# Rotary queries with channels on the partitions, their halves stacked by DMA

## The chip, the cores and the metric

The kernel runs on one core of a Trainium2 chip, in one launch. Its time is device microseconds; of several runs the median counts. Engines: PE (TensorE, matmuls and transposes), DVE (VectorE), ACT (ScalarE), POOL (GpSimd, here above all a queue of DMAs) and SP (SyncE, the other queue of DMAs). Each takes its instructions in the order in which they are written for it; they wait for one another by semaphores.

## The reference

Two layers of an encoder for 512 tokens of 2048 channels. Each layer normalises its input, projects it, and runs three kinds of head beside each other: latent attention (8 heads, 512 keys), a short gated convolution, and attention into 256 memory tokens (4 heads). What matters here is the rotary part of the latent queries, 64 channels of each head:

```python
def apply_rope(x, cos, sin):
    half = x.shape[-1] // 2
    x1, x2 = x32[..., :half], x32[..., half:]
    return jnp.concatenate([x1 * cos - x2 * sin, x2 * cos + x1 * sin], axis=-1)
...
q = (rmsnorm(q_lat, q_norm_g[l]) @ w_uq[l]).reshape(b, s, MLA_HEADS, QK_HEAD_DIM)
q = jnp.concatenate([q[..., :QK_NOPE_DIM],
                     apply_rope(q[..., QK_NOPE_DIM:], cos[:, :, None, :], sin[:, :, None, :])], axis=-1)
...
sc = jnp.einsum('bqhd,bkhd->bhqk', qi, k) * scale
m_out = memory_attention(q_mem, mem_n, w_mk[l], w_mv[l])
```

## The kernel before

All products are made in float32r; an operand that needs more bits is split in a high and a low part (`split_to`, L301: ACT casts the high part, the DVE subtracts it for the low part), and `mm3s` (L294) multiplies high by high, high by low and low by high: 12 matmuls for four blocks of channels and one PSUM bank.

The program is a list of Python steps (`add`, `put`) that are written one after the other. The order of PE, SP and POOL is that of the steps, by hand (L1488). The order of DVE and ACT is chosen by a scheduler when the program is built, except in the first steps and in the output projection. So a step that moves on PE moves what the scheduler makes of the other two.

`mixer` (L1124) writes, for each layer: the gates' transposes (tps, then y on ACT); in layer 0 beside them the keys and values of the memory (mk, mv, then Km, Vm); between these the rotary queries; then a pipeline (`pipeline`, L1104) of the four memory heads and the eight heads of latent attention. `head_iters` (L1029) gives each head four score tiles. A score tile goes: sc on PE, its negated maximum nm on the DVE (L1047), the exponential P on ACT (L1050), rec and the scaling of P, then three iterations later its transposes ptp on PE (L1067), the split into PT, and two iterations later the products o with the values (L298). Between the iterations stand the products of the next pair's queries (qps), keys (kps) and values (vps), with weights wh (ACT's cast, L212) and wl (DVE, L216).

The rotary queries (`q_rope_steps`, L918): for each of four token tiles t, `products(t)` makes a bank of 128 tokens x 512 (8 heads x 64 channels); `rot(t)` rotates it on the DVE (four rm of 128x256 with cos and sin, one sum, L946 to L950) and splits it into qs; `turn(t)` transposes qs on PE, eight 128x128 blocks (qrt, L971: a head's high part above its low part), and ACT copies them into the two tiles QR, four heads each (L973). `rot(2)` also has ACT compute an exponential of nothing (L960), so that the table of exponentials is loaded there (ACT_TABLE_LOAD) and not ahead of the first P. The rotary scores of latent attention read QR much later (L1043, L1044).

Buffers come in turn from pools: `raw` has 8 of 128x1024 f32 (4 KB a partition); the loaded weights (wr), rm and qs all take theirs from it. PSUM has 8 banks.

Of the kernel before, what the change touches and what calls it, by code (L numbers as in the profile page):

```python
# [5 lines left out]
F32 = mybir.dt.float32  # L6
# [3 lines left out]
ALU = mybir.AluOpType  # L10
# [241 lines left out]
def encoder(tc, x, mem, positions, pre_norm_g, w_in, q_norm_g, w_uq, kv_norm_g, w_ukv, conv_w,  # L252
# [665 lines left out]
    def q_rope_steps(l):  # L918
# [9 lines left out]
        units = [Unit(("qr", l, kp), [wl[:, 2 * kp + a, :, NOPE:] for a in range(2)], alloc=keep) for kp in range(2)]  # L928

        def products(t):  # L930
            def f(*ch):
                cH, cL = G["cq"]
                hi, lo = (a.rearrange("p (j c) -> p j c", j=4) for a in st["w"])
                ps = st["ps", t] = bank("qr")
                sl = slice(t * P, (t + 1) * P)
                mm3s([(ps, (cH[:, k, sl], cL[:, k, sl]), (hi[:, k, :], lo[:, k, :]), k == 0, k == 3, {})
                      for k in range(4)])
            return f

        def rotate(t, sc):  # L940
            q8 = st.pop(("ps", t)).rearrange("p (h s i) -> p h s i", h=HEADS, s=2)
            m1 = sc[:, :512].rearrange("p (h s i) -> p h s i", h=HEADS, s=2)
            m2 = sc[:, 512:].rearrange("p (h s i) -> p h s i", h=HEADS, s=2)
            cos, sin = G["cos2"][:, t], G["sin2"][:, t]
            for s in range(2):
                nc.vector.tensor_tensor(m1[:, :, s, :], q8[:, :, s, :],  # L946
                                        cos[:, s:s + 1, :].broadcast_to([P, HEADS, HALF]), op=ALU.mult)
                nc.vector.tensor_tensor(m2[:, :, s, :], q8[:, :, 1 - s, :],
                                        sin[:, s:s + 1, :].broadcast_to([P, HEADS, HALF]), op=ALU.mult)
            nc.vector.tensor_tensor(m1, m1, m2, op=ALU.add)  # L950
            return m1.rearrange("p h s i -> p h (s i)")

        def rot(t):
            def g():
                mr = rotate(t, raw_p.tile([P, 1024], F32, tag="raw", name=nm("rm")))
                qs = st["qs", t] = raw_p.tile([P, 1024], F32R, tag="raw", name=nm("qs")).rearrange(
                    "p (h s i) -> p h s i", h=HEADS, s=2)
                split_to(qs[:, :, 0, :], qs[:, :, 1, :], mr)
                if t == 2:
                    nc.scalar.activation(small(1, "nm"), mr[:, :1] if len(mr.shape) == 2 else mr[:, 0, :1], AF.Exp, scale=0.0)  # L960
            return g

        def turn(t):
            def g():
                if t == 0:
                    G["QR"] = [slab("QR", F32R).rearrange("p (h c) -> p h c", c=S) for _ in range(2)]
                qs = st.pop(("qs", t))
                for g4 in range(2):
                    pt = bank("qrt", F32R)
                    for h in range(4):  # L970
                        nc.tensor.transpose(pt[:, h * P:(h + 1) * P], qs[:, 4 * g4 + h].rearrange("p s i -> p (s i)"),  # L971
                                            G["identr"])
                    nc.scalar.copy(G["QR"][g4][:, :, t * P:(t + 1) * P],  # L973
                                   pt.bitcast(F32).rearrange("p (h c) -> p h c", h=4))
            return g
# [147 lines left out]

    def mixer(l, C, gates, pair2, tail):  # L1124

        rope, turns = q_rope_steps(l)
        if l == 0:
            ms = [(f, u, 1.0) for f, u, _ in mem_steps(l)]
            add(tables)
# [384 lines left out]
```

## Time and profile before

| | us |
|---|---|
| median of 3 runs | 1511.08 (1510.95 to 1511.76) |
| profiled execution | 1510.62 |
| its span, first to last instruction | 1508.8 |
| PE busy | 1485.1 (98%) |
| DVE busy | 1154.9 (77%) |
| ACT busy | 863.6 (57%) |
| POOL busy | 181.3 (12%) |

1.8 us of the profiled execution lie outside its span. The mean granted clock of PE over the span is 0.997 of full speed. The rotary queries of layer 0 are made from about 443 to 475 us, those of layer 1 from about 1192 to 1215 us. A row of a timeline gives the start of a run of like instructions and the time from its first start to its last end; matmuls overlap, so the time that a group holds PE is read from its start to the start of the next.

### The profile page before, as it was taken

The numbers are of one execution on the slowest core, as the hardware profiler recorded it, in microseconds if no ns is written. First come the engines' busy times: TensorE is split into PE (matmuls) and PEld (weight loads), VectorE is DVE, ScalarE is ACT, GpSimd is POOL, SyncE is SP. The second block draws the span as 40 slices with busy tenths as digits, with TensorE's granted clock in tenths as the row PEclk, the third lists the DMA queues.
The fourth block names the chain that finished last, engine by engine and source line by source line (L and its number), as shares of the span: only waits on it lengthen the run. The fifth ranks groups of instructions, "written<-read, shape, count | busy, mean of one in ns | idle before, by whom it ended". The sixth has DMA issues, their size and how long they took to land.

```text
span 1508.8 us, 20419 instructions
## 1 busy us (share of the span) xinstructions
PE 1485.1 (98%) x7613; PEld 1277.0 (85%) x7613; DVE 1154.9 (77%) x1516; ACT 863.6 (57%) x1327; POOL 181.3 (12%) x199
## 2 busy tenths in 40 slices
PE   8999999999999999999999999999999999999996
PEld 7878888997898888888888888888988888888875
DVE  5887877575887768888798877887686786698777
ACT  7743543454766768655498443534454686775534
POOL 0212020211000000021120112010221000002111
PEclk9999999999999999999999999999999999999998
DMA  8999695979565102399797899785978421127874
GB/s 308 226 219 220 188 193 165 193 198 239 164 212 166 43 29 68 94 214 283 220 343 230 225 231 225 199 179 156 207 198 202 158 76 37 43 89 147 283 177 128
DMA packets 144096, 270.64 MB, mean 179 GB/s; under 512 B 17160, under 2 KB 39788, under 8 KB 140780
## 3 DMA queue, kind: packets, MB, share of 16 engines
q1 hardware_dynamic: 108504, 190.10, 39.6%
q0 software_dynamic: 35360, 79.18, 27.0%
q8 instruction: 60, 0.98, 0.3%
q14 instruction: 40, 0.33, 0.1%
q10 hardware_dynamic: 132, 0.05, 0.0%
HBM read 254.61 MB, written 15.73 MB: 179 GB/s over the span
## 4 chain that ended last, share of the span: by engine, by line
PE 89%; DVE 3%; ACT 3%; DMA 2%; issue 2%; POOL 0%; DVEq 0%; POOLq 0%; ACTq 0%
PE P L298 62%; PE o L298 4%; PE mk L298 3%; PE mv L298 3%; PE qps L298 3%; PE ptp L1067 2%; PE tps L822 2%; PE vps L298 2%; PE qr L298 1%; PE kps L298 1%; PE sc L1039 1%; PE sc L1040 1%; PE sc L1045 1%; DMA wr<-in_w_in_dram 1%; PE sc L1044 1%
## 5 line engine op out<-in xcount | busy, mean ns | idle before, releaser
L212 ACT CAST wh<-wr 128x1024 fp32r<-128x1024 f32 (+1 forms) x404 | 413.5, 1031 | 449.3 <-PE P L298 258.9
L216 DVE TENSOR_TENSOR wl<-wr,wh 128x1024 fp32r<-128x1024 f32 (+1 forms) x404 | 479.1, 1194 | 223.2 <-ACT wh L212 219.2
L298 PE MATMUL P<-wh,S 128*128 128x512 f32 (+1 forms) x1792 | 444.9, 385 | 3.2 <-DVE S L435 1.5
L298 PEld LDWEIGHTS P<-wh,S 128*128 128x128 f32 x1792 | 334.3, 188 | 63.2 <-DVE S L435 1.9
L298 PE MATMUL P<-wh,A 128*128 128x512 f32 (+1 forms) x1312 | 325.8, 385 | 2.1 <-ACT wh L212 1.9
L298 PEld LDWEIGHTS P<-wh,A 128*128 128x128 f32 x1312 | 244.6, 188 | 47.5 <-ACT wh L212 3.2
L298 PE MATMUL P<-wl,S 128*128 128x512 f32 (+1 forms) x896 | 243.7, 384 | 0.0
L298 PEld LDWEIGHTS P<-wl,S 128*128 128x128 f32 x896 | 168.0, 188 | 30.5
L298 PE MATMUL P<-wl,A 128*128 128x512 f32 (+1 forms) x656 | 178.6, 384 | 0.1
L142 POOL DMA_DIRECT2D wr<-in_w_in_dram x84 | 101.7, 1212 | 550.2 <-DVE wl L216 458.8
L298 PEld LDWEIGHTS P<-wl,A 128*128 128x128 f32 x656 | 122.9, 188 | 22.6 <-DVE wl L216 0.5
L200 DVE TENSOR_TENSOR wr<-wr,wr 128x1024 f32<-128x1024 f32 (+1 forms) x100 | 118.9, 1191 | 10.1 <-DMA wr<-in_w_in_dram 7.9
L1050 ACT ACTIVATE P<-sc,nm 128x512 f32<-128x512 f32 (+1 forms) x96 | 59.8, 624 | 31.5 <-DVE nm L1047 30.8
L1047 DVE TENSOR_REDUCE nm<-sc 128x1 f32<-128x512 f32 (+1 forms) x96 | 57.0, 595 | 12.9 <-PE sc L1045 12.1
L303 DVE TENSOR_TENSOR PT<-ptp,PT 128x512 fp32r<-128x512 f32 (+1 forms) x96 | 56.6, 593 | 6.4 <-ACT PT L302 6.1
L142 POOL DMA_DIRECT2D wr<-in_w_o_dram x32 | 38.7, 1209 | 188.7 <-DVE wl L216 176.5
L1056 ACT ACTIVATE P<-P,rec 128x512 f32<-128x512 f32 (+1 forms) x80 | 53.9, 683 | 6.7 <-DVE rec L1052 6.7
L226 ACT ACTIVATE wh<-wr,cols 128x512 fp32r<-128x512 f32 x64 | 42.6, 715 | 21.5 <-PE mv L298 8.6
L302 ACT CAST PT<-ptp 128x512 fp32r<-128x512 f32 (+1 forms) x96 | 48.9, 521 | 9.3 <-PE ptp L1067 6.9
L298 PE MATMUL o<-PT,V 128*128 128x256 f32 x384 | 53.6, 289 | 0.0
L1067 PE MATMUL ptp<-identr,P 128*128 128x128 f32 x320 | 49.9, 272 | 0.8 <-ACT P L1056 0.7
L227 DVE SCALAR_TENSOR_TENSOR wl<-wr,cols,wh 128x512 fp32r<-128x512 f32 x64 | 45.2, 746 | 6.6 <-ACT wh L226 5.8
(256 smaller groups left out, 1758.2 us busy)
## 6 DMA issues: line engine op xcount, KB each, us to landing
wr<-in_w_in_dram SPq DMA_DIRECT2D x172, 512.0 KB, 4.5
wr<-in_w_o_dram SPq DMA_DIRECT2D x72, 512.0 KB, 4.1
wr<-in_w_in_dram POOLq DMA_DIRECT2D x68, 512.0 KB, 7.3
wr<-in_w_in_dram SPq DMA_DIRECT2D x40, 416.0 KB, 3.3
wr<-in_w_o_dram POOLq DMA_DIRECT2D x32, 512.0 KB, 7.7
wr<-in_w_mk_dram SPq DMA_DIRECT2D x16, 512.0 KB, 6.7
wr<-in_w_mv_dram SPq DMA_DIRECT2D x16, 512.0 KB, 5.8
wr<-in_w_in_dram POOLq DMA_DIRECT2D x16, 416.0 KB, 5.7
```

The lines of the kernel that those rows point to most:

```text
L142: engine.dma_start(dst, src, **kw)
L200: nc.vector.tensor_tensor(src, src, tiles[c], op=ALU.add)
L212: nc.scalar.copy(hi[:, :n], src)
L216: nc.vector.tensor_tensor(lo[:, :n], src, hi[:, :n].bitcast(F32), op=ALU.subtract)
L227: nc.vector.scalar_tensor_tensor(lo[:, h], src[:, h], g, hi[:, h].bitcast(F32), op0=ALU.mult, op1=ALU.subtract)
L298: nc.tensor.matmul(ps, a[turn[0]], b[turn[1]], start=first and turn == (0, 0), stop=last and turn == ((1, 0) if late == 0 else (0, 1)), **kw)
L302: nc.scalar.copy(hi, src)
L303: nc.vector.tensor_tensor(lo, src, hi.bitcast(F32), op=ALU.subtract)
L1047: nc.vector.tensor_reduce(nmax, ps, axis=AX.X, op=ALU.max, negate=True)
L1050: nc.scalar.activation(pt, ps, AF.Exp, bias=nmax, accum_out=tot)
L1056: nc.scalar.activation(pt, pt, AF.Copy, scale=rec)
L1067: nc.tensor.transpose(ps[:, k * P:(k + 1) * P], pt[:, k * P:(k + 1) * P], G["ident"])
```

## The change

A product bank now holds one half of the rotary channels (x = 0 the first 32 of a head's 64, x = 1 the last 32) of four heads (g = 0 or 1), 128 channels by 512 tokens: the weights are the stationary operand, the latent moves. There are again four banks of 12 matmuls a layer. `rot(g)` takes the two banks of a group of four heads and makes its two outputs, each with two products with a table, one sum or difference, and a split into qs, 128x512 throughout (L946 to L948, L303). The outputs lie with channels on the partitions already, so `turn` is gone; `stack(g)` brings high and low parts and the two halves into QR by DMA: for each x a copy of qs (512 KB) to DRAM (qsd, L963) and two reads of it into QR (256 KB each, L966), all on POOL's queue. The tables cos and sin are turned once in layer 0 (two copies on POOL, eight transposes on PE, two copies on ACT) and kept in DRAM (tabd) for layer 1, where SP loads them. The exponential of nothing moves to the end of `rot(1)` (L953). The rotary weights come in pieces of 32 channels, eight DMAs for four.

```diff
-        units = [Unit(("qr", l, kp), [wl[:, 2 * kp + a, :, NOPE:] for a in range(2)], alloc=keep) for kp in range(2)]
+        units = [Unit(("qr", l, kp), [wl[:, 2 * kp + a, :, NOPE + x * HALF:NOPE + (x + 1) * HALF] for a in range(2) for x in range(2)],
+                      alloc=keep) for kp in range(2)]
...
+        def products(g, x):
+            def f(*ch):
...
+                mm3s([(ps, (hi[:, k], lo[:, k]), (cH[:, k, :], cL[:, k, :]), k == 0, k == 3, {}) for k in range(4)], 0)
...
+        def rot(g):
+            def f():
+                one, two = st.pop(("ps", g, 0)), st.pop(("ps", g, 1))
+                cos, sin = st["tab"]
+                st["qs", g] = []
+                for a, b, op in ((one, two, ALU.subtract), (two, one, ALU.add)):
+                    m = raw_p.tile([P, 1024], F32, tag="raw", name=nm("rm"))
+                    nc.vector.tensor_tensor(m[:, :S], a, cos, op=ALU.mult)
+                    nc.vector.tensor_tensor(m[:, S:], b, sin, op=ALU.mult)
+                    nc.vector.tensor_tensor(m[:, :S], m[:, :S], m[:, S:], op=op)
+                    qs = raw_p.tile([P, 1024], F32R, tag="raw", name=nm("qs"))
+                    split_to(qs[:, :S], qs[:, S:], m[:, :S])
+                    st["qs", g].append(qs)
+                if g:
+                    nc.scalar.activation(small(1, "nm"), m[:, :1], AF.Exp, scale=0.0)
+            return f
+
+        def stack(g):
+            def f():
+                qr = slab("QR", F32R)
...
+                for x, qs in enumerate(st.pop(("qs", g))):
+                    d = dram.tile([P, 1024], F32, name=nm("qsd"))
+                    nc.gpsimd.dma_start(d, qs.bitcast(F32))
+                    for s in range(2):
+                        r = s * ROPE + x * HALF
+                        nc.gpsimd.dma_start(qr[r:r + HALF, :].rearrange("p (h c) -> p h c", c=S),
+                                            d[:, s * S:(s + 1) * S].rearrange("(h i) c -> i h c", i=HALF))
+            return f
...
-                    put(rope[q - 6], turns[q - 7:q - 6])
+                    put(rope[q - 6])
...
-            put(rope[2], turns[1:2], ms[14:15], rope[3], turns[2:3], ms[15:])
+            put(rope[2], stacks[:1], ms[14:15], rope[3], ms[15:], stacks[1:])
...
-                put([(g, []) for g in gates[2 * t:2 * t + 2]], rope[t])
-            put(turns[:1])
+                put([(g, []) for g in gates[2 * t:2 * t + 2]], rope[t], stacks[:1] if t == 2 else [])
+            put(stacks[1:])
...
-        for k, s in enumerate(turns[3:] if l == 0 else turns[1:]):
-            between[k] = between.get(k, []) + [s]
```

The rows that follow show the order of instructions on an engine; a name is a tile and its number, and the brackets name the semaphores waited for (DMASW: a DMA of POOL's queue has landed; DMAHW: one of SP's; else the engine).

The DVE in layer 1 before, around the first maximum of a memory score (nm_10647): rm_10584 and qs_10590 are token tile 2, rm_10620 is tile 3.

```order
L948 TENSOR_TENSOR rm_10584<-qr_10571,sin_3689 128x8x32
L950 TENSOR_TENSOR rm_10584<-rm_10584 128x512 [waits DVE_49]
L1047 TENSOR_REDUCE nm_10647<-sc_10643 128x1 [waits PE_49]
L303 TENSOR_TENSOR qs_10590<-rm_10584,qs_10590 128x8x64 [waits DVE_49,Activation_49]
L946 TENSOR_TENSOR rm_10620<-qr_10607,cos_3698 128x8x32 [waits DVE_49]
L948 TENSOR_TENSOR rm_10620<-qr_10607,sin_3689 128x8x32
```

The DVE in layer 1 after, at the same place (the first maximum is nm_10632): qs_10540 is output x = 1 of group 0, rm_10603 and qs_10607 are x = 0 of group 1, rm_10610 and qs_10614 its x = 1; wl_10751 are weights of the pair's keys and values.

```order
L303 TENSOR_TENSOR qs_10540<-rm_10536,qs_10540 128x512 [waits DMASW1_49,Activation_49]
L946 TENSOR_TENSOR rm_10603<-qr_10556,tab_10463 128x512 [waits DVE_49,PE_49]
L947 TENSOR_TENSOR rm_10603<-qr_10590,tab_10463 128x512 [waits PE_49]
L948 TENSOR_TENSOR rm_10603<-rm_10603 128x512 [waits DVE_49]
L216 TENSOR_TENSOR wl_10751<-wr_10355,wh_10750 128x1024 [waits DMAHW2_49,PE_49,Activation_49]
L303 TENSOR_TENSOR qs_10607<-rm_10603,qs_10607 128x512 [waits Activation_49]
L946 TENSOR_TENSOR rm_10610<-qr_10590,tab_10463 128x512 [waits DMASW4_49]
L947 TENSOR_TENSOR rm_10610<-qr_10556,tab_10463 128x512
L948 TENSOR_TENSOR rm_10610<-rm_10610 128x512 [waits DVE_49]
L1064 TENSOR_REDUCE nm_10632<-sc_10628 128x1
L303 TENSOR_TENSOR qs_10614<-rm_10610,qs_10614 128x512 [waits Activation_49]
```

The first maximum has moved behind the last rotation, and the second qs, the weights and the last rotation ahead of it wait for DMAs and for PE.

ACT in layer 1 before, from the table load to the first exponential of a score (P_10649).

```order
L960 ACT_TABLE_LOAD
L960 ACTIVATE nm_10593<-rm_10584 128x1 [waits DVE_49]
L973 CAST QR_10629<-qrt_10631 128x4x128 [waits PE_49]
L302 CAST qs_10590<-rm_10584 128x8x64 [waits PE_49]
L973 CAST QR_10630<-qrt_10637 128x4x128
L1050 ACTIVATE P_10649,tot_10650<-sc_10643,nm_10647 128x256 [waits DVE_49]
L302 CAST Q_10661<-qps_10662 128x512 [waits PE_49]
```

ACT in layer 1 after, up to the scaling of the first P (P_10634); L953 is the exponential of nothing.

```order
L302 CAST qs_10540<-rm_10536 128x512 [waits DMASW1_49,DVE_49,Activation_49]
L212 CAST wh_10750<-wr_10355 128x1024 [waits DMAHW2_49,PE_49]
L302 CAST qs_10607<-rm_10603 128x512 [waits DVE_49]
L302 CAST qs_10614<-rm_10610 128x512 [waits DVE_49,Activation_49]
L953 ACT_TABLE_LOAD
L953 ACTIVATE nm_10617<-rm_10610 128x1
L1067 ACTIVATE P_10634,tot_10635<-sc_10628,nm_10632 128x256 [waits DVE_49]
L1067 ACTIVATE P_10668,tot_10669<-sc_10662,nm_10666 128x256 [waits DVE_49]
L1073 ACTIVATE P_10634<-P_10634,rec_10637 128x256 [waits DVE_49]
```

The table load now stands behind the last qs cast, and the casts of Q, which stood between the first exponentials, come later.

POOL in layer 0 after, from the first copy of qs on: qs_3939 and qs_3946 are the two outputs of group 0, qs_4048 is the first of group 1.

```order
L963 DMA qsd_3983<-qs_3939 128x1024 [waits DMASW1_49,DVE_49]
L966 DMA QR_3982<-qsd_3983 32x4x512 [waits DMASW2_49,DMASW1_49,PE_49]
L966 DMA QR_3982<-qsd_3983 32x4x512 [waits DMASW3_49]
L963 DMA qsd_3987<-qs_3946 128x1024 [waits DMASW4_49,DVE_49]
L966 DMA QR_3982<-qsd_3987 32x4x512 [waits DMASW5_49,DMASW4_49]
L966 DMA QR_3982<-qsd_3987 32x4x512 [waits DMASW6_49]
L963 DMA qsd_4084<-qs_4048 128x1024 [waits DMASW7_49,DVE_49]
```

None of these DMAs was there before. The reads of a copy, which wait for its landing, stand ahead of the next copy in the same queue.

## Rows read from the trace of the kernel before

**Rows 1.** The page: busy time of each engine, and the chain that ended last.

```profile
PE 1485.1 (98%) x7613; PEld 1277.0 (85%) x7613; DVE 1154.9 (77%) x1516; ACT 863.6 (57%) x1327; POOL 181.3 (12%) x199
...
PE 89%; DVE 3%; ACT 3%; DMA 2%; issue 2%; POOL 0%; DVEq 0%; POOLq 0%; ACTq 0%
```

**Rows 2.** PE's waits, whole span (us in total, times, longest).

```profile
PE P L298 <- ACT wh L212: 2.8, 4, 0.9
...
PE ptp L1067 <- ACT P L1056: 0.7, 1, 0.7
```

**Rows 3.** Stretches: length, busy time (instructions) by engine, PE clock, DMA share, GB/s.

```profile
453.00:466.00 13.00, 13.00 (x81) 11.38 (x81) 8.25 (x15) 5.89 (x10) 0.41 (x5) 1.00 0.77 268
...
480.00:500.00 20.00, 19.30 (x140) 17.94 (x139) 18.81 (x55) 15.95 (x51) 0.00 (x0) 1.00 0.22 69
500.00:560.00 60.00, 60.00 (x361) 52.68 (x360) 39.16 (x74) 42.05 (x85) 0.00 (x0) 1.00 0.11 37
...
1219.00:1236.00 17.00, 16.92 (x124) 16.02 (x125) 15.99 (x48) 14.54 (x45) 0.00 (x0) 1.00 0.19 60
...
1485.00:1509.00 24.00, 11.27 (x50) 9.01 (x48) 16.37 (x24) 7.39 (x16) 4.44 (x6) 0.79 0.61 176
```

**Rows 4.** Timeline of PE, layer 1 (start, us, operation, repeats).

```profile
1198.70 1.03 PE L822 MATMUL tps<-identr,ga 128*128 128x128 f32 x8
...
1205.96 0.80 PE L971 MATMUL qrt<-identr,qs 128*128 128x128 f32 x8
1206.59 0.35 PE L1039 MATMUL sc<-Km,QmH 128*128 128x256 f32 x1
...
1219.24 0.95 PE L298 MATMUL o<-PT,Vm 128*128 128x256 f32 x6
```

**Rows 5.** Tiles rm, qs, QR: ns min/median/max, first to last start us.

```profile
L946 DVE TENSOR_TENSOR rm<-qr,cos x16: 410/416/426, 446.9 to 1209.0; 128x256 f32<-128x256 f32 x16
...
L303 DVE TENSOR_TENSOR qs<-rm,qs x8: 681/693/695, 450.4 to 1211.5; 128x512 fp32r<-128x512 f32 x8
...
L1043 PE MATMUL sc<-KAB,QR x64: 389/391/398, 497.3 to 1354.6; 128*128 128x512 f32 x64
```

**Rows 6.** Timelines of DVE and ACT, layer 1 ([idle before <- releaser]).

```profile
1201.78 0.69 DVE L303 TENSOR_TENSOR qs<-rm,qs 128x512 fp32r<-128x512 f32 x1 [0.74 <-ACT qs L302]
...
1207.21 0.42 DVE L1047 TENSOR_REDUCE nm<-sc 128x1 f32<-128x256 f32 x1 [2.49 <-PE sc L1045]
...
1215.31 1.23 DVE L216 TENSOR_TENSOR wl<-wr,wh 128x1024 fp32r<-128x1024 f32 x1 [0.77 <-ACT wh L212]
...
1204.06 1.28 ACT L960 ACT_TABLE_LOAD   x1
...
1207.93 0.49 ACT L1050 ACTIVATE P<-sc,nm 128x256 f32<-128x256 f32 x1
...
1214.19 1.09 ACT L212 CAST wh<-wr 128x1024 fp32r<-128x1024 f32 x1
...
1218.70 0.58 ACT L302 CAST K<-kps 128x512 fp32r<-128x512 f32 x1
1219.16 0.52 ACT L1056 ACTIVATE P<-P,rec 128x256 f32<-128x256 f32 x1
```

**Rows 7.** DMA issues (KB, median us to landing); landings of tiles xs and mTd.

```profile
xs<-xr POOLq DMA_DIRECT2D x8, 512.0 KB, 6.2
...
DMA to landing us min/median/max: 3.0/6.4/17.1
...
DMA to landing us min/median/max: 5.4/8.1/11.7
```

**Rows 8.** Timeline of PE, layer 0.

```profile
455.95 0.81 PE L971 MATMUL qrt<-identr,qs 128*128 128x128 f32 x8
...
479.53 0.38 PE L1067 MATMUL ptp<-identr,P 128*128 128x128 f32 x2
...
482.79 0.97 PE L298 MATMUL o<-PT,Vm 128*128 128x256 f32 x6
```

More of the change, by code (lines that the diff above doesn't have):

```diff
@@ L940, in rotate @@
[L940 to L975, printed above, removed]
@@ L976, in q_rope_steps @@
-        return [[(products(t), units if t == 0 else []), (rot(t), [])] for t in range(NT)], [(turn(t), []) for t in range(NT)]
+                hi, lo = (a.rearrange("p (k x g m) -> p k x g m", k=4, x=2, g=2)[:, :, x, g, :] for a in st["w"])
+                ps = st["ps", g, x] = bank("qr")
+                mm3s([(ps, (hi[:, k], lo[:, k]), (cH[:, k, :], cL[:, k, :]), k == 0, k == 3, {}) for k in range(4)], 0)
+            return f
+        def rot(g):
[14 more added lines that the diff above has]
+            return f
@@ new lines, in stack @@
+        def stack(g):
+            def f():
+                qr = slab("QR", F32R)
+                G["QR"] = G["QR"][:g] if g else []
+                G["QR"].append(qr.rearrange("p (h c) -> p h c", c=S))
+                for x, qs in enumerate(st.pop(("qs", g))):
[6 more added lines that the diff above has]
+            return f
@@ new lines, in tables_four @@
+        def tables_four():
+            if l:
+                tab = raw_p.tile([P, 1024], F32, tag="raw", name=nm("tab"))
+                nc.sync.dma_start(tab, G["tabd"])
+                st["tab"] = tab[:, :S], tab[:, S:]
+                return
+            st["four"] = [scrap(n) for n in ("cos4", "sin4")]
+            for v, src in zip(st["four"], (G["cos2"], G["sin2"])):
+                nc.gpsimd.tensor_copy(v.rearrange("p (t h i) -> p t h i", t=NT, h=4),
+                                      src[:, :, 1:, :].broadcast_to([P, NT, 4, HALF]))
@@ new lines, in tables_turn @@
+        def tables_turn():
+            tab = raw_p.tile([P, 1024], F32, tag="raw", name=nm("tab"))
+            st["tab"] = tab[:, :S], tab[:, S:]
+            for v, src in zip(st["tab"], st.pop("four")):
+                ps = bank("tab")
+                for t in range(NT):
+                    nc.tensor.transpose(ps[:, t * P:(t + 1) * P], src[:, t * P:(t + 1) * P], G["ident"])
+                nc.scalar.copy(v, ps)
+            G["tabd"] = dram.tile([P, 1024], F32, name="tabd")
+            nc.gpsimd.dma_start(G["tabd"], tab)
@@ L978, in qkv_steps @@
+        return ([[(products(g, x), units if g + x == 0 else [])] + ([(rot(g), [])] if x else []) for g in range(2)
+                 for x in range(2)], [(stack(g), []) for g in range(2)], (tables_four, tables_turn))
     def qkv_steps(l, pair, st):
@@ L1124, in mixer @@
     def mixer(l, C, gates, pair2, tail):
-        rope, turns = q_rope_steps(l)
+        rope, stacks, here = q_rope_steps(l)
         if l == 0:
```

10 lines of the change are left out of this document (4 added, 6 removed).

## The prediction

> **What bounds the kernel now.** I began with the totals and the chain of waits on the page. TensorE (PE) is busy 1485.1 us of a span of 1508.8, and the chain that ended last is 89% PE [rows 1]. Then the list of PE's waits: over the whole span its longest group is 2.8 us, and in the two stretches that the change touches there is one wait, 0.7 us [rows 2]. So PE is the bound, and almost nothing stands in its way. Two things follow. Work taken off PE there is worth its full length. And a new wait of PE there is lost for good, since no later stretch has room to catch up: from 500 to 560 us, in the first heads of latent attention, PE is busy 60.00 of 60 us [rows 3]. The same table shows who could become late: in the memory heads, behind the rotations, the VectorE (DVE) is busy 18.81 of 20 us (480 to 500) and 15.99 of 17 (1219 to 1236). There it can't make up a delay either. From 453 to 466, among the rotations, it is busy only 8.25 of 13 us [rows 3].
>
> **What PE loses.** Sixty-four 128x128 transposes (qrt) go, eight groups of eight. The first group of layer 1 starts at 1205.96 and the next matmul at 1206.59, so a group holds PE 0.63 us [rows 4]; eight of them are 5.1 us. Layer 0 gains eight transposes (tab). The nearest rows are that same 0.63 and eight tps, listed with 1.03 from the first start to the last end [rows 4]; I take 0.7, nearer the first, which is a spacing and so what the next matmul sees. The products stay 12 matmuls of 128x512 in each of eight banks; only which operand is stationary changes. Net on PE: -4.4 us; -1.8 in layer 0 (four groups of 0.63, less 0.7) and -2.5 in layer 1.
>
> **DVE and ScalarE (ACT) work.** Before, a token tile costs the DVE four rm of 0.41, a sum and a qs of 128x512, 0.69 each [rows 5]: 3.0 us, four times a layer, 12.1. After, an output costs two products, one sum and one qs, all 128x512; at 0.69 each, 2.8 us, four times, 11.0. ACT loses 16 casts of QR and gains two of tab. None of this decides, since the slack among the rotations covers it; what decides is the order.
>
> **The new order on DVE and ACT.** Before, the maximum of the first memory score (nm, 1207.21) comes right behind the third rotation, and ACT's table load stands ahead of it (1204.06); the exponential follows at 1207.93 [rows 6]. After, both stand behind the whole second rotation: the DVE's first nm behind rm of (g1, x1), ACT's table load behind the last qs cast. And three new waits sit in that row of work. The second qs takes the buffer that the first qs leaves, so it waits for the landing of the first copy to DRAM; the first product of (g1, x1) waits for the landing of the second copy; and wl, the weights of the next keys, now placed ahead of them, waits for the second qps. DVE and ACT take instructions in order: the score's nm, the exponentials, the casts of Q and PT all queue behind them, and PE waits for those at its first ptp and its first o.
>
> The price of a landing is not in the trace for these copies. The nearest row is the same form, 128x1024 from SBUF to DRAM, 512 KB, on the same queue (xs): median 6.2; all transfers into and out of that tile land in 3.0 at the least [rows 7]. Those of mTd, of twice the size, writes and reads together, have 5.4, 8.1 and 11.7 as least, median and most [rows 7]. I take 5.5 to 6, a little under the median of xs, which is the nearest form, and keep 3.0 and 8.1 as ends.
>
> A page speaks for the low end. In the Trainium skill, "DMA: Bandwidth & Descriptors", section "Anatomy of one DMA — SWDGE (gpsimd) path", a transfer from this queue costs about 2.0 us plus its bytes at 436 GB/s, which is an estimate of 3.2 us for 512 KB. The least landing in this trace agrees, the median of xs does not [rows 7]; by the page the time would be that of the fast-landing rival below.
>
> **Layer 1, on the clock of before.** The second bank of products ends at 1198.70 [rows 4]. Three DVE steps of (g0, x0) at 0.6 apart end at 1200.8, the cast by ACT leaves the DVE idle 0.74 [rows 6], the subtraction ends at 1202.2. Copy issued, landed at 1207.7. Only then the second qs: 1209.2. POOL, which has issued the two reads of the first copy meanwhile, sends the second; landed about 1215. Meanwhile rm of (g1, x0) ends at 1211.1. PE, without its transposes, runs from 1205.96: score 0.42, qps 2.76, two scores 0.84, qps 2.76, score 0.42, and wants ptp at 1213.2. ACT can take wh of the next weights only when the second qps has done with the old ones (1211.8), 1.09 us; wl on the DVE 1.23 [rows 6], to 1214.1; qs to 1214.8. So DMA and weights arrive together. rm of (g1, x1) 1215.0 to 1216.9, nm 1217.2. ACT: qs 0.62, the table load 1.28 and the small exponential behind it, two exponentials of 0.49, scaling 0.52 [rows 6], less what they overlap: P is ready at 1220.5. PE waits 7.3 us. Then the first o: on ACT four more exponentials, two scalings and two casts of Q stand in front, at 0.46 (the step from 1218.70 to 1219.16 [rows 6]) 3.7 us, then two casts of PT, and half a us goes on a wait for a late score: PT is there at 1225.2, its low part near 1226, where before o began at 1219.24 [rows 4]. Layer 1 loses 6.5 us to there, net of the transposes; with small waits behind it, as the DVE is full, I take 7.5. If the landings were 3.0, wl still holds the DVE to 1214.8, and only 0.2 is won; at 8.1 each the second lands at 1220.5, and 5.5 is added.
>
> **Layer 0.** Products end at 456.6 (before 455.95 [rows 8], plus 0.7 of tab). The first qs is done at 460.2, its copy lands at 466 (DMA share 0.77 from 453 to 466 [rows 3]). Here the second qs doesn't wait, but POOL does: it takes its DMAs in order, the reads of copy one stand ahead of copy two, so that goes out at 467.3 and lands at 473. rm of (g1, x1) to 475.1, nm 475.5, then ACT as above: P at 478.7, where PE wants it at 479.53 - 2.5 + 0.7 = 477.7 [rows 8]. The first o, behind the same casts and a wh of 1.09, at about 484.5; before 482.79 [rows 8]. That is +1.7, with landings a half us slower +2.7, and the waits behind it: I take 3.5. With landings of 3.0 nothing waits and the layer gains 1.8; with 8.1 it loses 8.
>
> **What I cost at nothing.** The reads into QR: the first rotary score of before is at 497.3 [rows 5], 20 us behind them, and heads 4 to 7 come later still; uncovered, each would cost a landing. The weights in eight pieces of 32 columns for four of 64: loaded six units ahead; uncovered, one landing more. POOL's two copies of the tables and the store of tabd: POOL is busy 181.3 us in all [rows 1].
>
> **Sum.** 3.5 + 7.5 = +11 on the profiled execution, whose 1510.62 us lie 0.5 under the median of the runs, 1511.08. Forecast: 1522.
>
> **Rivals.**
> Fast landings: both copies land near 3.0. Layer 0 gains 1.8, layer 1 still loses 7.3 to wl and the order: +5.5, 1516.5. For it: the least xs, and, with it, the queue's other least, 5.4 for twice the bytes [rows 7]. Against: the median.
> Slow landings: 8.1 each: 8 + 13 = +21, 1532. For it: mTd's median, and a DMA share of 0.77 in layer 0. Against: it takes four late landings out of four.
> PE's clock falls in the stall. From 1485 to 1509, where PE is busy 11.27 of 24 us, the granted clock is 0.79, against 1.00 in every other stretch of the table [rows 3]. Of 24 us at 2.4 GHz that means some 10 at 1.2 GHz. If as much follows the stall of layer 1 and half of it falls on work, 2.5 us are added: 1524.5 (up to 5 with no cover). The Trainium skill, "TensorE: Matmul & The Clock Gate", section "Part 1: The HAM clock gate", has the idle array drop to 1.2 GHz: it would make the waits cost more than their length. The trace's one such stretch agrees.
> The gain comes through: the first scores don't need to be early, because exponentials of later scores can run while PE does other work, and PE just drops its transposes: 1511.1 - 4.4 = 1506.7. For it: PE has 10.7 us of scores, qps and kps from 1205.96 to the first o, without the transposes [rows 4]. Against: the order puts those same exponentials behind the last rotation, and every landing and wl must then be early by more than 6 us in layer 1. It decides only if first nm starts before 1210.
>
> **How the numbers follow.** Both layers wait as forecast, with or without some slower clock: 0.64, its own range 1518 to 1527. Fast landings 0.12. Slow landings 0.12. The gain comes through 0.08; between these, by chance near zero, 0.04. About 0.2% (3 us) is what a measurement here can tell from no change. Slower 0.64 + 0.12 + 0.12 = 0.88, same 0.04, faster 0.08. The range reaches down past the fast landings and up to the slow ones: 1514 to 1531.
>
> **What would show it.** In the profile after: PE waits of several us at the first ptp of the memory heads, for ACT's P, and again at the first o, for PT or Q, larger in layer 1 than in layer 0; the DVE idle ahead of rm for a DMA; the first nm of layer 1 some 10 us behind its score; the table load right ahead of the first exponential; landings of qsd of 5 to 6 us. I am wrong if PE shows no wait of over 2 us there, if landings are near 3, or if the end moves down.

## The result and the profile after

| | before | after |
|---|---|---|
| median of the runs, us | 1511.01 (1509.47 to 1512.03) | 1521.28 (1519.13 to 1522.96) |
| ratio, 95% interval | | 1.0072 (1.0062 to 1.0082) |
| profiled execution, its span, us | 1510.62, 1508.8 | 1522.96, 1521.2 |
| mean granted clock of PE | 0.997 | 0.991 |

The kernel is slower by 10.3 us; the forecast was 11 (1522). The page's totals and chain after answer to [rows 1]:

```profile
PE 1486.3 (98%) x7557; PEld 1277.4 (84%) x7557; DVE 1155.4 (76%) x1500; ACT 857.8 (56%) x1313; POOL 196.1 (13%) x226
...
PE 90%; DVE 4%; ACT 3%; issue 2%; DMA 1%; POOL 0%; DVEq 0%; POOLq 0%; ACTq 0%
```

PE has 56 instructions fewer, yet is busy 1.2 us longer: part of its work ran at a lower clock. The list of PE's waits (us in total, times, longest), where [rows 2] had 0.7 us once, now begins with

```profile
PE ptp L1084 <- ACT P L1073: 9.8, 2, 8.0
```

The stretches of [rows 3] (length, busy time and instructions of PE, PEld, DVE, ACT, POOL, then PE's clock, DMA share, GB/s; the last is the tail, shifted with the end):

```profile
453.00:466.00 13.00, 13.00 (x79) 11.57 (x78) 8.10 (x13) 4.74 (x8) 2.34 (x5) 1.00 0.60 243
480.00:500.00 20.00, 16.68 (x111) 15.24 (x112) 16.25 (x48) 15.33 (x50) 2.91 (x9) 0.91 0.85 228
500.00:560.00 60.00, 60.00 (x363) 52.66 (x362) 41.10 (x80) 43.65 (x92) 0.00 (x0) 1.00 0.14 42
1219.00:1236.00 17.00, 9.83 (x49) 8.84 (x50) 12.73 (x35) 11.63 (x33) 2.20 (x4) 0.70 0.85 207
1497.00:1521.00 24.00, 11.04 (x49) 8.82 (x47) 16.14 (x24) 7.39 (x16) 4.43 (x6) 0.81 0.60 175
```

PE's busy time fell from 19.30 to 16.68 in the memory heads of layer 0 and from 16.92 to 9.83 in those of layer 1, and there the granted clock fell as well, to 0.91 and 0.70 on average, between its levels of 1.2 and 2.4 GHz. The window of layer 1 is the same stretch of time in both traces; after, everything in it comes 2.0 + 3.2 us later (below), and the wait covers 7 us of it. The next 60 us of layer 0 are full, as before: nothing is caught up.

PE's timeline after, for [rows 4] and [rows 8] (start, length, operation, repeats, and the idle time before it with its releaser): the turning of the tables, then layer 0's wait for the first ptp and the first o, then layer 1.

```profile
455.16 0.60 PE L987 MATMUL tab<-identr,cos 128*128 128x128 f32 x4
455.60 0.60 PE L987 MATMUL tab<-identr,sin 128*128 128x128 f32 x4
...
481.47 0.44 PE L1084 MATMUL ptp<-identr,P 128*128 128x128 f32 x2 [1.84 <-ACT P L1073]
...
485.18 0.44 PE L1084 MATMUL ptp<-identr,P 128*128 128x128 f32 x2 [0.38 <-ACT P L1067]
486.69 0.74 PE L298 MATMUL o<-PT,Vm 128*128 128x256 f32 x4 [1.07 <-ACT PT L302]
487.83 0.57 PE L298 MATMUL o<-PT,Vm 128*128 128x256 f32 x2 [0.41 <-DVE PT L303]
...
1214.94 1.09 PE L298 MATMUL qps<-cqH,wh 128*128 128x512 f32 x4
...
1226.17 0.69 PE L1084 MATMUL ptp<-identr,P 128*128 128x128 f32 x2 [7.97 <-ACT P L1073]
...
1228.36 1.91 PE L298 MATMUL kps<-ckv,wh 128*128 128x512 f32 x4
...
1232.25 0.96 PE L298 MATMUL o<-PT,Vm 128*128 128x256 f32 x6
...
1233.98 1.09 PE L298 MATMUL kps<-ckv,wh 128*128 128x512 f32 x4
```

Layer 1 waits 8 us at the first ptp and not at all at the first o: between them PE ran at half speed (the four kps at 1228.36 take 1.91 us, the same group at 1233.98 takes 1.09). Who made P late stands in the DVE's timeline of layer 1, for [rows 6]:

```profile
1208.28 0.69 DVE L948 TENSOR_TENSOR rm<-rm 128x512 f32<-128x512 f32 x1
1210.99 0.69 DVE L303 TENSOR_TENSOR qs<-rm,qs 128x512 fp32r<-128x512 f32 x1 [2.02 <-ACT qs L302]
...
1218.07 1.22 DVE L216 TENSOR_TENSOR wl<-wr,wh 128x1024 fp32r<-128x1024 f32 x1 [4.27 <-ACT wh L212]
1219.97 0.69 DVE L303 TENSOR_TENSOR qs<-rm,qs 128x512 fp32r<-128x512 f32 x1 [0.68 <-ACT qs L302]
1220.58 0.68 DVE L946 TENSOR_TENSOR rm<-qr,tab 128x512 f32<-128x512 f32 x1
...
1222.51 0.42 DVE L1064 TENSOR_REDUCE nm<-sc 128x1 f32<-128x256 f32 x1
```

The DVE stands idle 4.27 us ahead of wl; rm of (g1, x1) starts without a wait. POOL's queue in layer 1, which tells when a copy of [rows 7]'s kind had landed:

```profile
1210.87 1.12 POOL L966 DMA_DIRECT2D QR<-qsd  x2 [3.05 <-DMA qsd<-qs]
1211.97 0.55 POOL L963 DMA_DIRECT2D qsd<-qs  x1
1216.77 1.08 POOL L966 DMA_DIRECT2D QR<-qsd  x2 [4.24 <-DMA qsd<-qs]
```

The reads of copy 2 go out at 1216.77, so it had landed by then, 3.8 us before rm needed its buffer. Over all eight copies (the view of tile qs, whose only DMAs they are):

```profile
DMA to landing us min/median/max: 3.0/5.4/10.9
```

One by one, in order, they are 3.0, 8.6, 6.4 and 9.7 us in layer 0, 3.0, 4.5, 3.2 and 10.9 in layer 1; the first two of each layer, those of group 0, are the ones that can stand in the way of a rotation.

Where the time went, from marks in the two traces: from the latent's transposes to the first rotary score 100.36 us before and 103.60 after (+3.2, layer 0); from there to the last rotary score 857.55 and 865.36 (+7.8, layer 1). The first mark itself stands 2.0 us later after (398.90 for 396.94), ahead of anything that the change does; `e1_layer0`, with the same code there, has it at 396.83. That, and a tail shorter by 0.6, make up the 12.4 us between the two spans.

### The profile page after: what moved, and what is told of

Its sections match the earlier page's. It is cut to its first block, busy times and chain, and to the rows that moved or that the text cites. A ratio compares the mean times of both kernels' runs of the same rounds, so it can differ in the third digit from the quotient of the medians.

```text
span 1521.2 us, 20358 instructions
## 1 busy us (share of the span) xinstructions
PE 1486.3 (98%) x7557; PEld 1277.4 (84%) x7557; DVE 1155.4 (76%) x1500; ACT 857.8 (56%) x1313; POOL 196.1 (13%) x226
## 4 chain that ended last, share of the span: by engine, by line
PE 90%; DVE 4%; ACT 3%; issue 2%; DMA 1%; POOL 0%; DVEq 0%; POOLq 0%; ACTq 0%
PE P L298 63%; PE o L298 4%; PE mk L298 3%; PE mv L298 3%; PE qps L298 2%; PE ptp L1084 2%; PE tps L822 2%; PE vps L298 2%; PE kps L298 1%; PE qr L298 1%; PE sc L1056 1%; PE sc L1057 1%; PE sc L1062 1%; DMA wr<-in_w_in_dram 1%; PE sc L1061 1%
## 5 line engine op out<-in xcount | busy, mean ns | idle before, releaser
L303 DVE TENSOR_TENSOR PT<-ptp,PT 128x512 fp32r<-128x512 f32 (+1 forms) x96 | 56.3, 593 | 6.6 <-ACT PT L302 6.3
L1084 PEld LDWEIGHTS ptp<-identr,P 128*128 128x128 f32 x320 | 39.7, 142 | 18.3 <-ACT P L1073 10.2
```

The source lines that it names most:

```text
L303: nc.vector.tensor_tensor(lo, src, hi.bitcast(F32), op=ALU.subtract)
L1084: nc.tensor.transpose(ps[:, k * P:(k + 1) * P], pt[:, k * P:(k + 1) * P], G["ident"])
```

## The experiments

Each is compared with the kernel before, run beside it on the same chip (medians 1510.6 to 1511.9). Times are medians in us; the ratio to the kernel before, with its 95% interval, is the recorded one and can differ a little from the quotient of the medians.

### One layer at a time, and the gain alone

`e1_layer0` and `e2_layer1` use the changed code in one layer and the old code (as `q_rope_old`) in the other; in `e3_no_turns` the old rotation stays, the transposes and their casts go, and QR holds other data: it prices the transposes and computes something else.

```diff
+        if l == 0:
+            rope, stacks, here = q_rope_steps(l)
+        else:
+            rope, turns = q_rope_old(l)
```

```diff
+        if l == 0:
+            rope, turns = q_rope_old(l)
```

```diff
-                    pt = bank("qrt", F32R)
-                    for h in range(4):
-                        nc.tensor.transpose(...)
-                    nc.scalar.copy(G["QR"][g4][:, :, t * P:(t + 1) * P], ...)
+                if t == 0:
+                    for g4 in range(2):
+                        nc.gpsimd.dma_start(G["QR"][g4].rearrange("p h c -> p (h c)"), x[0][:P, :])
```

> The change in layer 0 alone; layer 1 turns its queries on PE as before. Theory: the loss lies in the waits of PE behind the late first maximum and in the slower clock behind them, layer by layer; in the two traces layer 0 loses 3.3 us and layer 1 7.8. So this kernel takes 1511.0 + 3.3 = 1514.3 us (1513 to 1516). Rival: the loss comes from the added DMA traffic (12 DMAs a layer through DRAM on POOL's queue) wherever it runs; the traffic is equal in the layers, so half of 10.3: 1516.2, and the same in e2.

> The change in layer 1 alone; layer 0 turns its queries on PE as before, and also makes the tables that layer 1 loads (8 transposes, 0.8 us of PE). Theory: 1511.0 + 7.8 + 0.8 = 1519.6 us (1518 to 1521), with one wait of PE of about 8 us at the first ptp of layer 1 and none over 1 us in layer 0. Rival (DMA traffic): 1511.0 + 5.2 + 0.8 = 1517.

> The kernel before without its 64 transposes of the queries and the 16 casts behind them (QR holds other data, brought by two DMAs a layer). It prices what the change takes off PE. Theory: PE is the bound, so the 5.0 us come through whole: 1511.0 - 5.0 = 1506.0 us (1505 to 1507). Rival: they were hidden beside a DVE that is nearly full in the memory heads, and little comes: 1509 to 1511.

Measured: `e1_layer0` 1513.04, ratio 1.0012 (1.0003 to 1.0021); `e2_layer1` 1518.67, 1.0051 (1.0039 to 1.0063); `e3_no_turns` 1506.17, 0.9961 (0.9949 to 0.9973); all three inside their ranges. So the transposes were worth what the forecast took. By the ratios layer 1 costs 7.7 us (5.9 to 9.5), with the turning of the tables, which stays in layer 0 (its marks give +0.9 there and +8.1 in layer 1), and layer 0 only 1.8 (0.5 to 3.2), half of its term. In `e1_layer0` PE has the same four waits at the same places as after, within 0.1 us:

```profile
479.50 0.44 PE L1144 MATMUL ptp<-identr,P 128*128 128x128 f32 x2 [1.94 <-ACT P L1133]
483.21 0.44 PE L1144 MATMUL ptp<-identr,P 128*128 128x128 f32 x2 [0.38 <-ACT P L1127]
484.71 0.74 PE L298 MATMUL o<-PT,Vm 128*128 128x256 f32 x4 [1.07 <-ACT PT L302]
485.86 0.50 PE L298 MATMUL o<-PT,Vm 128*128 128x256 f32 x2 [0.41 <-DVE PT L303]
```

but the clock of that stretch stayed whole:

```profile
480.00:500.00 20.00, 18.15 (x133) 16.56 (x132) 17.70 (x50) 16.99 (x51) 2.91 (x9) 1.00 0.79 212
```

Between the marks of layer 0 this trace has 102.17 us (396.83 to 499.00), 1.8 more than before, where that of after has 3.2 more. The other 1.4 us are the slow clock there: the waits over and PE full, it ran on about half clock for a while.

```profile
488.00:490.00 2.00, 2.00 (x11) 2.00 (x12) 1.78 (x7) 0.62 (x3) 0.00 (x0) 0.53 1.18 246
490.00:492.00 2.00, 2.00 (x7) 1.56 (x7) 1.18 (x4) 0.74 (x3) 0.00 (x0) 0.62 1.10 369
```

### The clock held

`e8_keep_clock` puts transposes of the identity, which nobody reads, into PE's wait (16 in layer 0, 76 in layer 1).

```diff
+                if j == 12 and t == 3:
+                    for k in range(WARM[len(warmed)]):
+                        nc.tensor.transpose(pb[:, MT + (k % 2) * P:MT + (k % 2 + 1) * P], G["ident"], G["ident"])
```

> The change with PE given something to do while it waits: transposes of the identity into an unused half of a bank, 16 in layer 0 and 76 in layer 1, ahead of the first ptp (they leave every result as it is). They fill most of the waits of 1.8 and 8.0 us, so the granted clock should stay at 1.00 behind them. Theory: the clock cost 1.5 us in layer 0 in those runs where it fell, and in layer 1 it mostly covers a wait for PT that then shows; 1 to 2.5 us are won: 1519.5 (1518.5 to 1520.5), with a wait at the first o of layer 1 of 1 to 2 us. Rival: the slower clock is a loss of its own beside the waits, 2 us in layer 0 and 2.5 in layer 1: 1516.8. Rival: the idle time itself doesn't lower the clock, and nothing changes: 1521.3.

Measured: 1521.03, 1.0066 (1.0053 to 1.0080), above the expected 1518.5 to 1520.5. In the profiled execution (1519.30) the clock is 1.00 in the memory heads of both layers, and the wait that the forecast put at the first o of layer 1 appears:

```profile
1227.77 0.74 PE L298 MATMUL o<-PT,Vm 128*128 128x256 f32 x4 [1.04 <-ACT PT L302]
1228.88 0.51 PE L298 MATMUL o<-PT,Vm 128*128 128x256 f32 x2 [0.37 <-DVE PT L303]
```

So part of PE's slow time after is waiting time told in another way, but not all of it. By the marks this trace loses 1.8 us in layer 0 (102.13) and 7.2 in layer 1 (864.73), that of after 3.2 and 7.8: in the profiled execution the slow clock cost about 2 us. The medians, 1521.03 and 1521.28, don't speak against it: two of the six executions of `e8_keep_clock` have a mean clock of 0.997 and take 1518.01 and 1519.30, the other four have 0.994 to 0.996 and take 1521.00 to 1523.06, so the transposes seem to have held the clock in some of them only. What the clock costs in the median is not shown.

### The order, in part and whole

`e5_table_early` only moves the exponential of nothing, and with it the table load, from the end of the rotation to behind the last gate. `e4_late_group` does that too, and makes group 1's products, rotation and stacking later, among the first heads of latent attention, where QR's second tile is not yet needed; layer 0 and layer 1 alike.

```diff
-                if g:
-                    nc.scalar.activation(small(1, "nm"), m[:, :1], AF.Exp, scale=0.0)
...
+        add(lambda: nc.scalar.activation(small(1, "nm"), G["ys"][1][:, 3, :1], AF.Exp, scale=0.0))
```

```diff
-            put(rope[2], stacks[:1], ms[14:15], rope[3], ms[15:], stacks[1:])
+            put(ms[14:15], stacks[:1], ms[15:])
...
+        for k, s in ((m - 4, [(here[2], [])]), (m + 1, rope[2]), (m + 3, rope[3]), (m + 5, stacks[1:])):
+            between[k] = between.get(k, []) + s
```

> The change with one instruction moved: the exponential of nothing, which loads ACT's table, hangs on the last gate and no longer on the last rotation (in both layers). Buffers and DMAs as in the change. The order then has the first maximum of layer 1 and the first exponential ahead of the second rotation. Theory: in-order queueing behind the second rotation made PE wait; the first ptp of layer 1 is then on time, and what is left is a wait of some 2 to 4 us at the first o, whose PT casts still stand behind the second rotation; layer 0, where the first maximum moves up by one instruction only, gains the table's 1.3 to 1.5 us. 1512 to 1515, I take 1513. Rival: the waits on the DVE for buffers and weights are what counts, and only the load itself goes from the path, 1.3 us a layer: 1518.

> The change with the second group of four heads made later: its products, rotation and DMAs stand among the first heads of latent attention, where the DVE has a third of its time free and which need it four heads later; the table of exponentials is loaded behind the last gate. The same products and the same DMAs, plus one load of the table a layer. Theory: nothing stands any more between the first memory score and its maximum, so PE's waits go and the saved transposes show: 1511.0 - 4.3 = 1506.7 us (1505 to 1509, the upper end if the second rotation makes PE wait in the latent heads). Rival (DMA traffic, or the landings): the traffic is all there and the time stays at 1516 to 1522.

Measured: `e5_table_early` 1515.64, 1.0031 (1.0020 to 1.0042), just above its range, and `e4_late_group` 1508.85, 0.9982 (0.9973 to 0.9990), inside it. The table load's place is half of the loss, not by the 1.28 us that it takes but by the order: the scheduler no longer holds every exponential behind the last rotation. ACT in layer 1 of `e5_table_early`, where the first exponential runs 7 us ahead of the first qs cast of group 1:

```profile
1205.34 1.28 ACT L1168 ACT_TABLE_LOAD   x1
...
1208.43 0.47 ACT L1065 ACTIVATE P<-sc,nm 128x256 f32<-128x256 f32 x1 [1.09 <-DVE nm L1062]
...
1215.43 0.62 ACT L302 CAST qs<-rm 128x512 fp32r<-128x512 f32 x1 [1.29 <-DVE wl L216]
```

With group 1 out of the way as well all of the loss is gone, and 2.9 us of the transposes' gain come through: `e4_late_group` is faster than both kernels. It has all the DMAs of the change, so their traffic alone isn't the loss. (Group 1 made later with the table load left in its place was not run.) PE's waits at ptp in `e4_late_group` are two of 0.7, and the two stretches are full at whole clock:

```profile
480.00:500.00 20.00, 20.00 (x134) 18.30 (x134) 16.35 (x47) 15.52 (x45) 0.00 (x0) 1.00 0.37 82
1219.00:1236.00 17.00, 17.00 (x106) 15.21 (x105) 13.55 (x34) 12.57 (x34) 0.00 (x0) 1.00 0.33 74
```

### Weights or landings

`e6_own_buffers` gives qs a buffer from another pool (`slab`, that of Q, K, PT and QR), so that no step of the rotation waits for a copy to land; `e7_both` is that with the early table load. `e9_weights_own` gives layer 1's first key weights a buffer of their own, so that they don't wait for the second qps. `e10_slow_copies` sends two more copies ahead of each.

```diff
-                    qs = raw_p.tile([P, 1024], F32R, tag="raw", name=nm("qs"))
+                    if op == ALU.subtract:
+                        both = slab("qs2", F32R)
+                    qs = both[:, :1024] if op == ALU.subtract else both[:, 1024:]
```

```diff
+        def own():
+            w = slab("kw", F32R)
+            return w[:, :1024], w[:, 1024:]
+        ku = Unit(("ukv", l, pair), alloc=own if l and not pair else None, loads=[...])
```

```diff
+                    for k in range(2):
+                        nc.gpsimd.dma_start(dram.tile([P, 1024], F32, name=nm("qsx")), qs.bitcast(F32))
```

> The change with qs in buffers of its own (one slab for the two outputs of a group) instead of the ring that it shares with rm and the weights: no DVE or ACT instruction waits any more for a copy to land, and in the built order the weights of the next keys (wl) move behind the first maxima. The table load stays behind the last rotation. Same DMAs. Theory: the buffer reuse gave the DVE its waits; without it the rotations of layer 1 end some 6 us earlier and P comes when PE wants it: both layers about even with before or up to 2 us better, 1510 to 1513, I take 1511. Rival: the table load alone matters, and it is still in its place: 1518 or more. Rival: DMA traffic: 1520.

> Both of the last two edits: qs in its own buffers and the table loaded behind the last gate. Theory: no new wait is left in front of the memory heads, and the saved transposes show, less small waits at the first o of each layer: 1507 to 1510, I take 1508. Rival: the second rotation still costs the DVE 5 us ahead of stretches where it is full, and PE pays some of it: 1511 or more.

> The changed kernel, with one difference: in layer 1 the weights of the first pair's keys and values lie in a buffer of their own, so that ACT's cast (wh) and the DVE's low part (wl) no longer wait for PE's second qps. The landings of the copies to DRAM and the order on DVE and ACT stay. Theory: in layer 1 the DVE waited 4.3 us for these weights ahead of the last rotation, while the second copy had landed 3.8 us before it was needed. So the weights alone set the delay there: the wait at the first ptp of layer 1 falls from 8.0 us to about 4, and the time from 1521.3 to about 1517.5 (1516.5 to 1519). Rival: the landings are as late as the weights, as the forecast had it (DMA and weights arrive together): the wait stays near 8 us and the time near 1521. A caution: in the kernel with own buffers for qs the wait came back at the first o, since the buffers were taken from the pool of PT and Q; if that happens here, the first ptp is earlier, the first o waits for PT, and the time is near 1521 as well.

> The changed kernel with two more copies of the same size (512 KB, into DRAM that nobody reads) ahead of each copy of qs on POOL's queue, so that each real copy lands later. Theory: in layer 0 the second copy landed in the same moment as its buffer was needed (1475.82 against 475.88 us, a tie), so all of the delay goes on the wait at the first ptp there; in layer 1 the second copy had 3.8 us to spare, so only what goes beyond that does. With some 3 us more for each extra copy, two copies one behind the other on the path in layer 0 make about 10 us there, in layer 1 6 to 10 us: 1521.3 + 17 = about 1538 (1530 to 1548). Rival: the wait comes from the order on DVE and ACT and from the weights alone, and the landings have no part in it: 1521 to 1524, with the DVE waiting for nothing longer than now.

(The last means 475.82 and 475.88.) Measured: `e6_own_buffers` 1520.83, 1.0064 (1.0052 to 1.0076); `e7_both` 1521.02, 1.0063 (1.0051 to 1.0076): both expectations failed. `e9_weights_own` 1517.82, 1.0052 (1.0040 to 1.0065), as expected in time, but by other waits. `e10_slow_copies` 1529.35, 1.0118 (1.0103 to 1.0134), slower, but by half of what was expected and not in the way expected.

In `e9_weights_own` the wait at the first ptp of layer 1 fell from 8.0 to 1.5, where about 4 was expected, and a new one stands at the first o. PE:

```profile
1216.34 0.44 PE L1088 MATMUL ptp<-identr,P 128*128 128x128 f32 x2 [1.50 <-ACT P L1077]
...
1223.69 1.74 PE L298 MATMUL o<-PT,Vm 128*128 128x256 f32 x6 [3.20 <-ACT PT L302]
```

The cause is on ACT. In the changed kernel six exponentials and three scalings of P stand between the table load and the first cast of Q in layer 1; here seven and four, the seventh waits for its maximum, and the cast wh, which the changed kernel has ahead of the last rotation, stands among them:

```profile
1218.10 1.04 ACT L212 CAST wh<-wr 128x1024 fp32r<-128x1024 f32 x1
...
1220.83 0.47 ACT L1071 ACTIVATE P<-sc,nm 128x256 f32<-128x256 f32 x1 [0.82 <-DVE nm L1068]
...
1221.62 0.51 ACT L1077 ACTIVATE P<-P,rec 128x256 f32<-128x256 f32 x1 [0.23 <-DVE rec L1073]
1222.04 1.05 ACT L302 CAST Q<-qps 128x512 fp32r<-128x512 f32 x2
```

The same seven and four, wh among them, stand in the timelines of `e6_own_buffers` and `e7_both`, with waits at the first o of layer 1 of 2.95 and 3.40. Both kernels wait there a second time, at a later o (2.93 and 2.70), behind a cast for which ACT stood idle 3.92 and 3.50 us with no releaser in the profile; of `e6_own_buffers`:

```profile
1235.09 0.59 ACT L302 CAST V<-vps 128x512 fp32r<-128x512 f32 x1 [3.92 <-issue]
```

In `e10_slow_copies` the seven and four stand in both layers, with waits of 3.15 and 3.14; in layer 0 the changed kernel has wh among its six and three too, and waits 1.07 there. At the first ptp `e10_slow_copies` waits as long as the changed one does (layer 1):

```profile
1232.05 0.69 PE L1086 MATMUL ptp<-identr,P 128*128 128x128 f32 x2 [8.04 <-ACT P L1075]
```

although its first copy landed late enough to hold the DVE 4.72 us instead of 2.02; the wait for the weights behind it shrank from 4.27 to 1.21. So in layer 1 the first copy has slack. Of the second copy it is no test in either layer: with the extra copies the buffers took other turns, and no rotation waited for it. In layer 1 the last one started before it had landed:

```profile
1226.50 0.69 DVE L946 TENSOR_TENSOR rm<-qr,tab 128x512 f32<-128x512 f32 x1
```

```profile
1228.46 1.12 POOL L968 DMA_DIRECT2D QR<-qsd  x2 [6.32 <-DMA qsd<-qs]
```

`e9_weights_own` isn't a test of the weights alone either: the free buffer also took the wait for copy 2 away. There rm starts at 1210.79 and the reads behind copy 2 go out at 1213.52, so with that wait kept the first ptp would come up to 2.7 us later and wait about 4 (an estimate from these two times). That the weights, and not copy 2, held the last rotation of the changed kernel rests on that copy's 3.8 us of slack in its trace.

### ACT in the written order, and buffers in part

After these, a new theory: the wait at the first o is ACT's order. `e11_act_written` is `e7_both` with ACT's instructions of the memory heads in the order of the steps; `e12_mixed` is the same with group 1's qs back in the first pool.

```diff
+            if k == 0:
+                add(lambda: act.enter_context(tc.manual_schedule(engines={mybir.EngineType.Activation})))
+            if k == 16:
+                add(act.close)
```

```diff
...
+                    if g:
+                        qs = raw_p.tile([P, 1024], F32R, tag="raw", name=nm("qs"))
+                    else:
+                        qs = both[:, :1024] if op == ALU.subtract else both[:, 1024:]
```

> The kernel with both edits (own buffers for qs, the exponential of nothing behind the last gate), which measured 1521, and in it ACT's instructions of the memory heads in the order in which the steps are written: an exponential, the casts of Q when their products are there, a transposed tile's cast behind its transpose. The scheduler no longer sets that order; it still sets the DVE's. Theory, new after those runs: the wait at the first o came from ACT's order, in which a seventh exponential and a fourth scaling stood ahead of the casts of Q and PT (six and three in the changed kernel). Then the waits at the first o go (9.9 us in all before), and the time falls to about 1510 (1507 to 1516: the third PT of a head takes the buffer of group 1's copies, the last of which may land up to 4 us late). Rival: the wait comes from the buffers, since PT and Q take over those whose copies to DRAM land late: then the waits at o stay and the time is near 1521.

> As the kernel with ACT's order written, but only the first group's qs have a buffer of their own; those of group 1 lie where the changed kernel has them. So no PT, K or Q waits for a copy of group 1, and no rotation for a copy of group 0. Theory (order on ACT and DVE is all that is left): no wait of PE over 1 us in the two stretches, 1507.5 (1506 to 1510), a gain of about 4 on the kernel before, near what the kernel without transposes had (1506.2), with the rotation still ahead of the heads. Rival (the buffers of group 1 matter as well): the time equals that of the kernel with all qs in own buffers, or is above 1512.

Measured: `e11_act_written` 1524.96, 1.0090 (1.0076 to 1.0104), and `e12_mixed` 1515.29, 1.0029 (1.0017 to 1.0041). Both times missed, and yet both sides of the question are answered. With ACT in the written order the wait at the first o of `e7_both` falls from 3.4 to 0.43 in layer 1: that one was the order. But the buffers matter as well, as the rival said. In `e11_act_written` (layer 1) POOL waits for the buffer of the second QR until a score lets go, so copy 4 leaves at 1234.81; a later PT takes over the buffer of group 1's qs and waits for it; and PE waits for the exponentials behind that cast:

```profile
1233.73 1.09 POOL L966 DMA_DIRECT2D QR<-qsd  x2 [11.88 <-PE sc L1062]
1234.81 0.56 POOL L963 DMA_DIRECT2D qsd<-qs  x1
1239.76 1.08 POOL L966 DMA_DIRECT2D QR<-qsd  x2 [4.39 <-DMA qsd<-qs]
```

```profile
1239.53 0.37 ACT L302 CAST PT<-ptp 128x256 fp32r<-128x256 f32 x1 [4.80 <-issue]
```

```profile
1240.43 0.58 PE L1056 MATMUL sc<-Km,QmH 128*128 128x256 f32 x1 [3.99 <-ACT P L1067]
```

(The profile names no releaser for ACT's 4.80 us; the cast starts when POOL's reads of copy 4 could, so I take it for that landing.) In `e12_mixed` these are gone. Most of what is left waits for the DVE's scaling of P, which the scheduler still puts behind the last rotation (layer 1; 1.8 in layer 0):

```profile
1218.81 0.69 PE L1087 MATMUL ptp<-identr,P 128*128 128x128 f32 x2 [3.24 <-DVE P L1074]
```

## Why the prediction was right, step by step

**The transposes.** 5.0 us of qrt (eight times 0.63; the forecast's 5.1 and its net of 4.4 are 0.1 too high) less 0.7 for the tables. Right: the kernel without them is 5.5 faster (its casts are gone too), and the tables hold PE 0.79 us (455.16 to the next product at 455.95).

**The weights in layer 1.** Right, and more than the forecast gave them: "DMA and weights arrive together" failed. Copy 2 landed 3.8 us ahead, and wl, behind the second qps, was what the last rotation stood behind. Without that wait, and without the one for copy 2, the first ptp waits 1.5 us instead of 8.0. So one sign named ahead, the DVE idle ahead of rm for a DMA, is not there; the first nm did come 11 us behind its score.

**Landings of 5.5 to 6.** Right in the median only, 5.4 of 3.0 to 10.9. The two copies on the path took 3.0 and 8.6 us in layer 0, 3.0 and 4.5 in layer 1. In layer 1 that changed nothing, since the weights came later still. In layer 0 the two make 11.6, what the forecast gave them together: luck. In the Trainium skill, "DMA: Bandwidth & Descriptors", section "Anatomy of one DMA — SWDGE (gpsimd) path", the estimate was 3.2; three of the eight (3.0, 3.0 and 3.2) agree. In layer 0 copy 2 took 8.9 us from its issue at 466.90 to the reads behind it, and ended where wl, Vm and qs on the DVE ended as well (475.82 against 475.88): a tie, so the forecast's queue behind the reads was right, but not alone.

**First ptp and first o.** The first wait of layer 1 was forecast at 7.3 and is 8.0. The wait at the first o was forecast for both layers; in layer 0 it is there (1.07 and 0.41), in layer 1 half clock hides it, and with the clock held it is there (1.04 and 0.37).

**Layer 0, +3.5.** The term that was mis-sized: 1.8 by the ratio and by the trace of `e1_layer0`, with 3.8 us of waits less 1.8 of net gain. The part that was worked out, +1.7 at the first o, was right (some 2 us, counted from the first mark); the 1.8 put on it for slower landings and for waits behind the first o did not come. The trace of after has 3.2, because in that execution the clock fell there too. Layer 1, +7.5, measured 7.7 with the tables' turning by the ratio, 7.8 in the trace of after and 7.2 with the clock held.

**The clock.** It fell in the stall, as that rival said, and in the profiled execution it cost some 2 us (the rival: 2.5), 0.6 in layer 1 and 1.4 in layer 0, where the forecast didn't look for it. The sum had no term for it. So that 1522 came so near is in part luck: layer 0 was put 1.7 us too high, and a slow clock of about that size was left out. With the clock held the two layers lose 9.0 us in the trace and not 11. What of it is in the median, 1521.3, stays open.

**What was costed at nothing.** Right: no wait of PE for QR or for the rotary weights is in the list after.

**The gain comes through.** That rival fails for the order as it was: with rotation and table load ahead of the first maximum, PE has nothing to do. It holds for another order of the same work, `e4_late_group`.

Shown by runs: the table load's place (half of the loss), and with it the rotation of group 1 ahead of the first heads (all of it). Read from the trace, and borne out by a run only together with copy 2: the weights behind the second qps. Open: what of layer 0 is DMA and what is weights, since no run parted them there, and the clock's price in the medians.

## What to carry to other kernels

A step that takes work off the bounding engine must be priced by what it puts ahead of the next critical instruction on the in-order engines; here 4 us of transposes went, exponentials, maxima and casts got late, and the kernel lost 10 us net. Look for work whose result is needed late, and move it out of the row instead of giving it more buffers: of the eight kernels that were to lessen the loss only that one beat both. A buffer from another pool didn't end a wait here, it handed it to whoever took the buffer next, and each change of buffers made the scheduler choose a new order, so read the order again before believing the time. And a forecast that lands on the number can hold two errors that cancel: compare it term by term.

## What was not expected of the hardware

The same four waits within 8 us left PE's clock whole in one execution (1.00 in `e1_layer0`) and brought it down in another (0.91 after), and there only when they were over and PE was full (0.53 from 488 to 490 us). In the Trainium skill, "TensorE: Matmul & The Clock Gate", section "Part 1: The HAM clock gate", the idle array falls to 1.2 GHz; the long wait of layer 1 agrees (0.70), these short ones only sometimes. And copies of one size on one queue landed between 3.0 and 10.9 us in one kernel, the longest beside a DMA share of 0.85.
